# Gate 7 finished before group 5 is turned, and SSM groups 6 and 7 used last in the output projection

## The chip, the core and the metric

The kernel runs on one core of one Trainium2 chip. The metric is the device time of one execution in microseconds (us). Three runs of the kernel before gave 777.24, 779.81 and 781.50 us, median 779.81 us. TensorE (PE) does the matrix products and transposes, ScalarE (ACT) and VectorE (DVE) do elementwise work from SBUF and PSUM, GpSimd (POOL) does elementwise work on SBUF alone, and SyncE (SP) issues the weight transfers.

## The reference, cut to what matters

The whole kernel is a two-layer decoder trunk over 256 tokens of width 1024: a Mamba-2 SSD mixer with a gated feed-forward block, then dilated attention with another one. The change touches the end of the mixer only:

```
z, xbc, dt  = split(h @ w_in)
xs, B, C    = silu(conv(xbc) + conv_b)            # 8 groups: xs 256 wide, B and C 128 wide
y           = ssd(xs, dt, a, B, C) + xs * d_skip  # per chunk of 128 tokens:
              #   cb = C B^T;  y_diag = (cb * decay) (xs*dt);  y_off = C * state of the chunk before
y           = y * silu(z)                         # the gate
y           = y * rsqrt(mean(y*y over its group)) * norm_w
x           = x + y @ w_out                       # 2048 -> 1024
```

Each group has 256 of the 2048 channels of y, which are two of the 16 blocks of 128 over which `y @ w_out` sums. Blocks 12 and 13 are group 6, blocks 14 and 15 are group 7.

## The kernel before

All products are taken in three terms of split fp32 operands: high times high, high times low, low times high. Weights come as 1 MB blocks into a ring of three raw buffers; ACT casts each half to its high part (`split`, line 96, tile wh) and DVE subtracts to get the low part (line 98, tile wl), both in rings of six. PE's instructions run in the order in which the code is written; on ACT, DVE, POOL and SP a scheduler sets one order at build time, and each of these engines then works through its own list in that order.

The SSM loop runs over groups g = 0 to 7. In each turn PE makes xs (`conv_mm(g, "xs")`), B and C (`conv_mm(g, "bc")`), and in the odd turns 1, 3, 5 and 7 also one gate tile of 256 channels (`ZAT`), in two halves of 24 products (`z_mm(g, 0)` and `z_mm(g, 1)`, lines 290 to 292) that `z_post` sends through a Silu. The other steps of a group are spread over later turns:

- `ssd_b(g)`: PE transposes xs (tile px, line 542), DVE makes xdt and xd from it, POOL the third part of xdt (line 551).
- `ssd_a(g)`: PE makes C B^T (tile pg, lines 519 and 520) from B and C after their Silu (line 416), ACT copies it to gs (lines 524, 525).
- `ssd_m(g)`: POOL multiplies the decay tile dec by gs in two halves (line 531).
- `ssd_c(g)`: PE makes yo and py (lines 560 and 565, py from dec), then DVE line 567, POOL line 570, DVE line 571, POOL line 572 (times the gate), ACT line 575 (squares), DVE 576, POOL 578 (the power -0.5) and ACT line 580 (times the result) give the normed tile y2.
- `ssd_d(g)`: PE turns y2 (tile pt, line 588), ACT and DVE make the high and low part yy from it (lines 186 and 187), the operand of the output projection.

In turn 7 PE does xs, half of bc, `ssd_d(4)`, `ssd_c(5)`, the other half of bc, `ssd_b(6)`, `ssd_a(6)`, then `z_mm(7, 0)`, `ssd_d(5)`, `ssd_c(6)`, `z_mm(7, 1)`, and after the loop `ssd_b(7)` and `ssd_a(7)`. `ssd_d(6)`, `ssd_c(7)` and `ssd_d(7)` are hung into the output projection as hooks.

`res_proj` does the output projection. Its first four output tiles run together: for each half of the 16 blocks it goes tile by tile and does one step for each block that isn't in the list `late`; a step is three products (lines 666 to 668). The blocks in `late` come last, block by block over the four tiles. Hooks are called after so many steps, or ahead of a late block (`"k12"`). So before, with blocks 14 and 15 late, there are 56 steps and then 8 late ones; `ssd_d(6)` comes after step 20, `ssd_c(7)` after 24, `ssd_d(7)` after 52.

Of the kernel before, what the change touches and what calls it, by code (L numbers as in the profile page):

```python
# [16 lines left out]
NG = 8  # L17
# [10 lines left out]
ZAT = {1: 4, 3: 5, 5: 6, 7: 7}  # L28
# [25 lines left out]
def trunk(ctx, tc, a, out):  # L54
# [428 lines left out]
    yy = []  # L483
# [28 lines left out]
    def z_post(g):  # L512
        seq(out=gate(g), in_=sts[g]["poz"], func=AF.Silu)
# [23 lines left out]
    def ssd_b(g):  # L537
        st = sts[g]
        px = ps.tile([128, 2, T], F32, tag="t1", name="px")
        for c in range(2):  # L540
            for i in range(2):
                PE.transpose(px[:, c, i * 128:i * 128 + 128], st["xs"][:, i, c * 128:c * 128 + 128], ident)
        h4 = slice(4 * g, 4 * g + 4)
        xdt = wk.tile([128, 3, T], F32, tag="B", bufs=3, name="xdt")
        DVE.tensor_tensor(out=hd(xdt[:, 0:2, :]), in0=hd(px),
                          in1=dts[:, :, h4].unsqueeze(3).to_broadcast([128, 2, 4, 64]), op=ALU.mult)
        xd = wk.tile([128, 2, T], F32, tag="B", bufs=3, name="xd")
        DVE.tensor_tensor(out=hd(xd), in0=hd(px),
                          in1=P("dskip")[:, h4].unsqueeze(1).unsqueeze(3).to_broadcast([128, 2, 4, 64]),
                          op=ALU.mult)  # L550
        POOL.tensor_tensor(out=hd(xdt[:, 2:3, :]), in0=hd(xdt[:, 0:1, :]),
                           in1=ea[:, 32 + 4 * g:36 + 4 * g].unsqueeze(1).unsqueeze(3)
                           .to_broadcast([128, 1, 4, 64]), op=ALU.mult)
        st["xdt"], st["xd"] = xdt, xd

    def ssd_c(g):
        st = sts[g]
        d, xdt, xd, gs = dec[g], st["xdt"], st["xd"], st["gs"]
        po = ps.tile([128, 512], F32, tag="t4", name="yo")[:, :T]
        PE.matmul(po, lhsT=gs[:, 2, :], rhs=xdt[:, 2, :], start=True, stop=True)  # L560
        py = ps.tile([128, 2, T], F32, tag="t2", name="py")
        for c in range(2):
            for j in range(4):
                f = slice(64 * j, 64 * j + 64)
                PE.matmul(py[:, c, f], lhsT=d[:, j, c, :], rhs=xdt[:, c, f], start=True, stop=True)  # L565
        y2 = act.tile([128, 2, T], F32, tag=f"dec{g}", name="y2")
        DVE.tensor_tensor(out=hd(y2[:, 1:2, :]), in0=hd(po.unsqueeze(1)),
                          in1=ea[:, 4 * g:4 * g + 4].unsqueeze(1).unsqueeze(3).to_broadcast([128, 1, 4, 64]),
                          op=ALU.mult)
        POOL.tensor_tensor(out=xd[:, 1, :], in0=xd[:, 1, :], in1=y2[:, 1, :], op=ALU.add)  # L570
        DVE.tensor_tensor(out=xd, in0=py, in1=xd, op=ALU.add)
        POOL.tensor_tensor(out=y2, in0=xd, in1=gate(g), op=ALU.mult)
        sm = wk.tile([128, 2], F32, tag="sm", name="sm")
        for c in range(2):
            ACT.activation(out=xd[:, c, :], in_=y2[:, c, :], func=AF.Square, accum_out=sm[:, c:c + 1])
        DVE.tensor_scalar(out=sm, in0=sm, scalar1=1.0 / 256, scalar2=GEPS, op0=ALU.mult, op1=ALU.add)
        rs = wk.tile([128, 2], F32, tag="rs", name="rs")
        POOL.tensor_tensor(out=rs, in0=sm, in1=nhalf, op=ALU.pow)
        for c in range(2):
            ACT.activation(out=y2[:, c, :], in_=y2[:, c, :], func=AF.Copy, scale=rs[:, c:c + 1])  # L580
        st["y2"] = y2

    def ssd_d(g):
        st = sts[g]
        y2, pt = st["y2"], ps.tile([128, 2, T], F32, tag="t5", name="pt")
        for i in range(2):
            for c in range(2):
                PE.transpose(pt[:, i, c * 128:c * 128 + 128], y2[:, c, i * 128:i * 128 + 128], ident)
        y = act.tile([128, 4, T], F32R, tag=f"dec{g}", name="yy")
        for i in range(2):  # L590
            hi_lo(y[:, 2 * i, :], y[:, 2 * i + 1, :], pt[:, i, :], P("ssm_norm")[:, 2 * g + i:2 * g + i + 1])
        yy.append(y)
# [5 lines left out]
    for g in range(NG):  # L598
        for i in range(2):
            conv_mm(g, "xs", i)  # L600
        conv_post(g, "xs")
        conv_silu(g, "xs")
        conv_mm(g, "bc", 0)
        if g == 0:
            chunk_sums()
            decay_load(0)
            decay_load(1)
        if g > 2:
            ssd_d(g - 3)
        if g > 1:  # L610
            ssd_c(g - 2)
        conv_mm(g, "bc", 1)
        conv_post(g, "bc")
        if g and g % 2 == 0:
            decay_load(g)
            decay_load(g + 1)
        if g % 2 == 0:
            decay(g, sts[g]["end"])
            decay(g + 1, sts[g]["end"])
        if g:  # L620
            ssd_b(g - 1)
            ssd_a(g - 1)
            ssd_m(g - 1)
        conv_silu(g, "bc")
        if g == 0:
            seq(out=ea, in_=acs[:, 32:96], func=AF.Exp)
        if g % 2 == 0:
            decay_exp(g)
            decay_exp(g + 1)
        if g in ZAT:  # L630
            z_mm(ZAT[g], 0)
            if g == NG - 1:
                ssd_d(g - 2)
                ssd_c(g - 1)
            z_mm(ZAT[g], 1)
            z_post(ZAT[g])
    ssd_b(NG - 1)
    ssd_a(NG - 1)
    ssd_m(NG - 1)

    def res_proj(w, nk, operand, late, S, first=2, hooks={}):

        done = [0] * KT
        po, units = {}, {}

        def step(n, k):  # L650
            wh, wl = units[n, k // 8]
            c = slice((k % 8) * 128, (k % 8) * 128 + 128)
            shared, wide = n < first > 2, n >= (first if first > 2 else 0) and nk > AH
            if n not in po:
                po[n] = po[n - 1] if shared and n % 2 else acc_bank()
            y, p = operand(k), po[n]
            st, sp = done[n] == 0, done[n] == nk - 1
            done[n] += 1
            if wide:
                PE.matmul(p.rearrange("p c t -> p (c t)"), lhsT=wh[:, c], rhs=y.rearrange("p c t -> p (c t)"),  # L660
                          start=st, stop=False, skip_group_check=True)
                PE.matmul(p[:, 1, :], lhsT=wl[:, c], rhs=y[:, 0, :], start=False, stop=sp,  # L662
                          skip_group_check=True)
            else:

                o = n % 2 if shared else 0
                for q, (l, x) in enumerate(((wh, 0), (wh, 1), (wl, 0))):
                    PE.matmul(p[:, o, :], lhsT=l[:, c], rhs=y[:, x, :], start=st and q == 0 and not o,  # L668
                              stop=sp and q == 2, skip_group_check=True)
            if sp and shared:  # L670
                if n % 2:
                    for q in range(2):
                        finish(n - 1 + q, [p[:, q, :]])
            elif sp:
                finish(n, [p[:, q, :] for q in range(1 + wide)])

        def finish(n, ys):
            x = X[:, n, :]
            for y in ys:
                DVE.tensor_tensor(out=x, in0=y, in1=x, op=ALU.add)  # L680
            S.add(n)

        n0, steps = 0, 0
        while n0 < KT:
            m = first if n0 == 0 else 2
            tiles = range(n0, n0 + m)
            last = late if n0 == 0 else []
            for b in range(0, nk, 8):
                for p in range(n0 // 2, (n0 + m) // 2):
                    units[2 * p, b // 8], units[2 * p + 1, b // 8] = W.get(w, p, b)  # L690
                for n in tiles:
                    for k in range(b, min(b + 8, nk)):
                        if k not in last:
                            step(n, k)
                            steps += 1
                            hooks.get(steps, int)()
            for k in last:
                hooks.get(f"k{k}", int)()
                for n in tiles:
                    step(n, k)  # L700
            n0 += m

    S = Stream(["ffn_norm0"])
    res_proj("w_out", 16, lambda k: yy[k // 2][:, k % 2 * 2:k % 2 * 2 + 2, :], [14, 15], S,
             first=4, hooks={20: lambda: ssd_d(NG - 2), 24: lambda: ssd_c(NG - 1), 52: lambda: ssd_d(NG - 1)})


    def ffn(L, S, nxt):
# [251 lines left out]
    S = Stream(["ffn_norm1"])  # L960
# [209 lines left out]
```

## Time and profile before

| | |
|---|---|
| three runs, median (range) | 779.81 us (777.24 to 781.50) |
| the profiled execution's own time | 777.25 us |
| its span, first to last instruction | 775.5 us |
| PE busy (share of the span) | 761.5 us (98%) |
| DVE, ACT, POOL busy | 604.4, 470.1, 146.2 us |
| granted TensorE clock, mean | 0.997 of full speed (2.4 GHz) |

The span lies 1.75 us below the time of its own execution. Matmuls are pipelined: one of 256 columns is shown with 0.28 us though the next one starts 0.12 us later, so what a stretch costs is read from starts, not from the sum of durations. "Idle before" in a row counts from the shown end of the instruction ahead.

### The profile page before, as it was taken

Reading aid. Unit: us, or ns where it says so; the run is one execution under the profiler, and the core shown is the slowest. Engines: PE = TensorE matmul, PEld = TensorE weight load, DVE = VectorE, ACT = ScalarE, POOL = GpSimd, SP = SyncE. Lnnn points to the kernel's source line nnn. Section 1 sums busy time; section 2 is a strip of 40 time slices with the busy share of each in tenths; the row PEclk is TensorE's granted clock in tenths of the full one; section 3 lists DMA queues with packets and bytes.
Section 4 is the critical chain, followed back from the end, with each engine's and each line's share of the span. In section 5 each row is a group of like instructions: output and inputs, shape, how many; then the busy total and the mean of one; then the engine's idle time right before and its main releaser. Section 6 shows DMA issues by size and latency. Waiting matters only on the chain.

```text
span 775.5 us, 14630 instructions
## 1 busy us (share of the span) xinstructions
PE 761.5 (98%) x5832; PEld 721.9 (93%) x5832; DVE 604.4 (78%) x1008; ACT 470.1 (61%) x793; POOL 146.2 (19%) x142
## 2 busy tenths in 40 slices
PE   8999999989999999999999999999999999999996
PEld 7899999989989999999888998989999999999885
DVE  5989988887496999887677598777587999888452
ACT  6757777775566676565556446556376767655331
POOL 0003626354216100000111132111125200000000
PEclk9999999999999999999999999999999999999998
DMA  8584753434173565545556554253234565554621
GB/s 308 212 300 170 283 174 110 164 109 158 61 272 110 173 233 202 207 151 173 184 200 236 194 189 147 101 187 118 105 115 158 191 224 212 184 197 141 220 75 54
DMA packets 22772, 135.72 MB, mean 175 GB/s; under 512 B 2544, under 2 KB 3600, under 8 KB 8624
## 3 DMA queue, kind: packets, MB, share of 16 engines
q1 hardware_dynamic: 21216, 130.03, 48.2%
q10 hardware_dynamic: 1488, 4.75, 1.8%
q8 instruction: 46, 0.75, 0.4%
q14 instruction: 22, 0.18, 0.1%
HBM read 133.17 MB, written 1.61 MB: 174 GB/s over the span
## 4 chain that ended last, share of the span: by engine, by line
PE 89%; DVE 4%; issue 2%; ACT 2%; DMA 1%; POOL 1%; SPq 0%; POOLq 0%; DVEq 0%
PE po L270 18%; PE po L271 17%; PE po L272 17%; PE po L660 7%; PE po L668 4%; PE po L662 4%; PE fo L1030 2%; PE fo L1028 2%; PE fo L1029 2%; PE py L565 2%; DVE wl L98 2%; PE po L290 1%; PE po L291 1%; PE po L292 1%; DMA raw<-w_z 1%
## 5 line engine op out<-in xcount | busy, mean ns | idle before, releaser
L98 DVE TENSOR_TENSOR wl<-raw,wh 128x1024 fp32r<-128x1024 f32 (+1 forms) x238 | 296.2, 1250 | 77.9 <-ACT wh L96 73.8
L96 ACT CAST wh<-raw 128x1024 fp32r<-128x1024 f32 (+1 forms) x238 | 245.0, 1040 | 184.3 <-PE po L271 99.1
L270 PE MATMUL po<-xnh,wh 128*128 128x256 f32 x800 | 226.6, 283 | 0.0
L272 PE MATMUL po<-xnh,wl 128*128 128x256 f32 x800 | 226.1, 283 | 0.0
L271 PE MATMUL po<-xnl,wh 128*128 128x256 f32 x800 | 225.3, 282 | 0.0
L270 PEld LDWEIGHTS po<-xnh,wh 128*128 128x128 f32 x800 | 150.9, 189 | 0.4 <-issue 0.2
L271 PEld LDWEIGHTS po<-xnl,wh 128*128 128x128 f32 x800 | 151.0, 189 | 0.0
L272 PEld LDWEIGHTS po<-xnh,wl 128*128 128x128 f32 x800 | 150.1, 188 | 0.1
L270 PE MATMUL po<-xh,wh 128*128 128x256 f32 x400 | 114.7, 287 | 0.0
L271 PE MATMUL po<-xl,wh 128*128 128x256 f32 x400 | 113.0, 282 | 0.5 <-DVE xl L187 0.5
L272 PE MATMUL po<-xh,wl 128*128 128x256 f32 x400 | 113.1, 283 | 0.0
L314 DVE SCALAR_TENSOR_TENSOR cv<-po,prm,cv 128x255 f32<-128x255 f32 (+2 forms) x232 | 106.2, 477 | 5.4 <-ACT cv L310 2.8
L270 PEld LDWEIGHTS po<-xh,wh 128*128 128x128 f32 x400 | 76.1, 190 | 1.6 <-issue 1.5
L271 PEld LDWEIGHTS po<-xl,wh 128*128 128x128 f32 x400 | 76.1, 190 | 0.7 <-DVE xl L187 0.7
L272 PEld LDWEIGHTS po<-xh,wl 128*128 128x128 f32 x400 | 75.8, 190 | 0.0
L660 PE MATMUL po<-gp,wh 128*128 128x512 f32 x176 | 61.4, 392 | 0.0
L230 POOL TENSOR_TENSOR sqacc<-sqacc,sq 128x256 f32<-128x256 f32 x21 | 21.4, 1019 | 211.5 <-ACT sq L229 211.2
L662 PE MATMUL po<-gp,wl 128*128 128x256 f32 x176 | 49.3, 280 | 0.0
L660 PEld LDWEIGHTS po<-gp,wh 128*128 128x128 f32 x176 | 33.0, 187 | 7.5
L1028 PE MATMUL fo<-wh,gp 128*128 128x512 f32 x88 | 34.5, 392 | 0.0
L1030 PE MATMUL fo<-wl,gp 128*128 128x512 f32 x88 | 34.5, 392 | 0.0
L1029 PE MATMUL fo<-wh,gp 128*128 128x512 f32 x88 | 34.5, 392 | 0.0
(226 smaller groups left out, 1283.0 us busy)
## 6 DMA issues: line engine op xcount, KB each, us to landing
raw<-w_up SPq DMA_DIRECT2D x44, 1024.0 KB, 4.8
raw<-w_down SPq DMA_DIRECT2D x18, 1024.0 KB, 4.8
raw<-w_xs SPq DMA_DIRECT2D x8, 1024.0 KB, 6.2
raw<-w_bc SPq DMA_DIRECT2D x8, 1024.0 KB, 5.5
raw<-w_out SPq DMA_DIRECT2D x8, 1024.0 KB, 4.9
raw<-w_q SPq DMA_DIRECT2D x8, 1024.0 KB, 5.1
raw<-w_z SPq DMA_DIRECT2D x6, 1024.0 KB, 6.0
dec<-rows ACTq DMA_DIRECT2D x8, 512.0 KB, 5.3
```

The lines of the kernel that those rows point to most:

```text
L96: ACT.copy(out=wh[:, :n], in_=raw)
L98: DVE.tensor_tensor(out=wl[:, :n], in0=raw, in1=wh[:, :n].bitcast(F32), op=ALU.subtract)
L270: PE.matmul(po, lhsT=wh, rhs=xh, start=start, stop=False, **kw)
L271: PE.matmul(po, lhsT=wh, rhs=xl, start=False, stop=False, **kw)
L272: PE.matmul(po, lhsT=wl, rhs=xh, start=False, stop=stop, **kw)
L314: r = DVE.scalar_tensor_tensor(out=dst[:, i, s:], in0=u[:, i, :T - s], scalar=w[i][:, taps - 1 - s:taps - s], in1=dst[:, i, s:], op0=ALU.m ...
L660: PE.matmul(p.rearrange("p c t -> p (c t)"), lhsT=wh[:, c], rhs=y.rearrange("p c t -> p (c t)"), start=st, stop=False, skip_group_check=True)
L662: PE.matmul(p[:, 1, :], lhsT=wl[:, c], rhs=y[:, 0, :], start=False, stop=sp, skip_group_check=True)
L668: PE.matmul(p[:, o, :], lhsT=l[:, c], rhs=y[:, x, :], start=st and q == 0 and not o, stop=sp and q == 2, skip_group_check=True)
L1028: PE.matmul(po[c], lhsT=x[:, 0, t], rhs=wh[:, o], start=k == 0, stop=False)
L1029: PE.matmul(po[c], lhsT=x[:, 1, t], rhs=wh[:, o], start=False, stop=False)
L1030: PE.matmul(po[c], lhsT=x[:, 0, t], rhs=wl[:, o], start=False, stop=k == FT - 1)
```

## The change

Two edits, with every instruction of the computation kept. In turn 7 both halves of gate 7 are made together, and `ssd_d(5)` and `ssd_c(6)` come behind them, ahead of `ssd_b(7)`. In the output projection blocks 12 and 13 join the late ones, and the three hooks move: `ssd_c(7)` still after step 24 and now first, `ssd_d(6)` after step 30, `ssd_d(7)` ahead of late block 12. There are now 48 steps and then 16 late ones.

```diff
-        if g in ZAT:
+        if g in ZAT and g < NG - 1:
             z_mm(ZAT[g], 0)
-            if g == NG - 1:
-                ssd_d(g - 2)
-                ssd_c(g - 1)
             z_mm(ZAT[g], 1)
             z_post(ZAT[g])
+    z_mm(7, 0)
+    z_mm(7, 1)
+    z_post(7)
+    ssd_d(NG - 3)
+    ssd_c(NG - 2)
     ssd_b(NG - 1)
     ssd_a(NG - 1)
     ssd_m(NG - 1)
...
-    res_proj("w_out", 16, lambda k: yy[k // 2][:, k % 2 * 2:k % 2 * 2 + 2, :], [14, 15], S,
-             first=4, hooks={20: lambda: ssd_d(NG - 2), 24: lambda: ssd_c(NG - 1), 52: lambda: ssd_d(NG - 1)})
+    res_proj("w_out", 16, lambda k: yy[k // 2][:, k % 2 * 2:k % 2 * 2 + 2, :], [12, 13, 14, 15], S,
+             first=4, hooks={24: lambda: (ssd_c(NG - 1),), 30: lambda: (ssd_d(NG - 2),), "k12": lambda: (ssd_d(NG - 1),)})
```

PE between the two halves of gate 7, before (y2_1996 is the normed tile of group 5, po_2061 the gate's bank):

```order
L291 MATMUL po_2061<-wh_1947,xnl_335 128x256
L292 MATMUL po_2061<-wl_1949,xnh_334 128x256
L588 MATMUL pt_2096<-cst_76,y2_1996 128x128 x4
L560 MATMUL yo_2106<-xdt_2047,gs_2055 128x256
L565 MATMUL py_2108<-xdt_2047,dec_1838 128x64 x8
L290 MATMUL po_2061<-wh_1943,xnh_334 128x256
L291 MATMUL po_2061<-wh_1943,xnl_335 128x256
```

The same place of PE in the changed kernel, behind the last product of the gate's second half:

```order
L291 MATMUL po_2061<-wh_1947,xnl_335 128x256
L292 MATMUL po_2061<-wl_1949,xnh_334 128x256
L588 MATMUL pt_2121<-cst_76,y2_1996 128x128 x4
L560 MATMUL yo_2131<-xdt_2047,gs_2055 128x256
L565 MATMUL py_2133<-xdt_2047,dec_1838 128x64 x8
L542 MATMUL px_2155<-cst_76,cv_1930 128x128 x4
L519 MATMUL pg_2165<-cv_2033 128x256
L520 MATMUL pg_2165<-cv_2033 128x128
L670 MATMUL po_2193<-yy_1070,wh_2064 128x256 x2
```

The turning of group 5 and yo and py of group 6 stand 24 products later, and px and pg of group 7 follow them directly.

ACT from the norm of group 5 on, before (cv is B and C of group 7, y_2117 group 6, zp gate 7):

```order
L580 ACTIVATE y_1996<-y_1996,rs 128x256 x2
L525 COPY gs<-pg 128x128
L96 CAST wh<-raw 128x1024
L186 ACTIVATE yy<-pt,prm 128x256 x2
L416 ACTIVATE cv<-cv 128x512
L96 CAST wh<-raw 128x1024
L575 ACTIVATE xd,sm<-y_2117 128x256 x2
L416 ACTIVATE zp<-po 128x2x256
```

ACT from the same place in the changed kernel (y_2142 is group 6):

```order
L580 ACTIVATE y_1996<-y_1996,rs 128x256 x2
L525 COPY gs<-pg 128x128
L96 CAST wh<-raw 128x1024 x3
L186 ACTIVATE yy<-pt,prm 128x256
L416 ACTIVATE cv<-cv 128x512
L416 ACTIVATE zp<-po 128x2x256
L186 ACTIVATE yy<-pt,prm 128x256
L524 COPY gs<-pg 128x256
L525 COPY gs<-pg 128x128
L575 ACTIVATE xd,sm<-y_2142 128x256 x2
```

Two more casts of weights stand ahead of the Silu of B and C of group 7.

POOL at groups 6 and 7, as a difference (y_2117 and y_2142 are group 6 before and now, y_2288 and y_2278 group 7; the dec rows and xdt are group 7):

```order
-L570 TENSOR_TENSOR xd<-xd,y_2117 128x256
-L572 TENSOR_TENSOR y_2117<-xd,zp 128x512
+L570 TENSOR_TENSOR xd<-xd,y_2142 128x256
+L531 TENSOR_TENSOR dec<-dec,gs 128x512
+L551 TENSOR_TENSOR xdt<-xdt,ea 128x256
+L531 TENSOR_TENSOR dec<-dec,gs 128x512
+L572 TENSOR_TENSOR y_2142<-xd,zp 128x512
 L578 TENSOR_TENSOR rs<-sm,nhalf 128x2
-L551 TENSOR_TENSOR xdt<-xdt,ea 128x256
-L531 TENSOR_TENSOR dec<-dec,gs 128x512 x2
```

The three POOL instructions of group 7 now stand inside group 6's chain, between lines 570 and 572.

## Rows read from the trace of the kernel before

**Rows 1.** Waits of PE over the span, longest group: total us, times, longest

```profile
PE pt L588 <- ACT y L580: 2.1, 1, 2.1
```

**Rows 2.** Timeline of PE, turn 7: start us, duration us, line, tiles, count [idle before]

```profile
168.92 0.36 PE L290 MATMUL po<-wh,xnh 128*128 128x256 f32 x1
...
174.07 0.95 PE L588 MATMUL pt<-cst,y 128*128 128x128 f32 x4 [2.09 <-ACT y L580]
...
177.36 0.36 PE L290 MATMUL po<-wh,xnh 128*128 128x256 f32 x1
...
180.29 0.60 PE L542 MATMUL px<-cst,cv 128*128 128x128 f32 x4
180.73 0.60 PE L519 MATMUL pg<-cv 128*128 128x256 f32 x2
...
181.30 0.49 PE L668 MATMUL po<-yy,wh 128*128 128x256 f32 x2
```

**Rows 3.** Timeline of PE: group 4 turned, group 5's yo and py, no wait

```profile
162.38 0.60 PE L588 MATMUL pt<-cst,y 128*128 128x128 f32 x4
...
164.95 0.36 PE L270 MATMUL po<-xnh,wh 128*128 128x256 f32 x1
```

**Rows 4.** Timeline of ACT, turn 7 and output projection

```profile
173.51 0.91 ACT L580 ACTIVATE y<-y,rs 128x256 f32<-128x256 f32 x2 [0.26 <-POOL rs L578]
...
174.47 1.05 ACT L96 CAST wh<-raw 128x1024 fp32r<-128x1024 f32 x1
175.42 0.47 ACT L186 ACTIVATE yy<-pt,prm 128x256 fp32r<-128x256 f32 x1
176.51 0.47 ACT L186 ACTIVATE yy<-pt,prm 128x256 fp32r<-128x256 f32 x1 [0.62 <-DVE yy L187]
176.89 0.63 ACT L416 ACTIVATE cv<-cv 128x512 f32<-128x512 f32 x1
...
184.16 0.90 ACT L580 ACTIVATE y<-y,rs 128x256 f32<-128x256 f32 x2
...
198.83 0.91 ACT L580 ACTIVATE y<-y,rs 128x256 f32<-128x256 f32 x2 [1.34 <-POOL rs L578]
```

**Rows 5.** Timeline of DVE, turn 7 and output projection

```profile
176.39 0.47 DVE L314 SCALAR_TENSOR_TENSOR cv<-po,prm,cv 128x253 f32<-128x253 f32 x1
...
177.66 0.42 DVE L567 TENSOR_TENSOR y<-yo,ea 128x256 f32<-128x256 f32 x1 [0.80 <-PE py L565]
...
179.55 3.43 DVE L98 TENSOR_TENSOR wl<-raw,wh 128x1024 fp32r<-128x1024 f32 x2
...
184.29 1.23 DVE L98 TENSOR_TENSOR wl<-raw,wh 128x1024 fp32r<-128x1024 f32 x1
...
193.03 0.42 DVE L567 TENSOR_TENSOR y<-yo,ea 128x256 f32<-128x256 f32 x1
```

**Rows 6.** Timeline of POOL, groups 6 and 7

```profile
173.44 2.51 POOL L531 TENSOR_TENSOR dec<-dec,gs 128x512 f32<-128x512 f32 x2
...
179.78 2.12 POOL L572 TENSOR_TENSOR y<-xd,zp 128x512 f32<-128x512 f32 x1 [0.87 <-DVE xd L571]
...
183.80 0.62 POOL L551 TENSOR_TENSOR xdt<-xdt,ea 128x256 f32<-128x256 f32 x1
...
185.40 3.53 POOL L531 TENSOR_TENSOR dec<-dec,gs 128x512 f32<-128x512 f32 x2 [0.98 <-ACT gs L524]
```

**Rows 7.** Timeline of PE in the output projection, at the hooks

```profile
188.59 0.60 PE L588 MATMUL pt<-cst,y 128*128 128x128 f32 x4
188.94 0.48 PE L668 MATMUL po<-yy,wh 128*128 128x256 f32 x2
...
190.46 0.60 PE L560 MATMUL yo<-xdt,gs 128*128 128x256 f32 x2
...
192.59 0.48 PE L668 MATMUL po<-yy,wh 128*128 128x256 f32 x2
...
202.74 0.60 PE L588 MATMUL pt<-cst,y 128*128 128x128 f32 x4
```

## The prediction, made before the changed kernel ran

> **What bounds the kernel now.** I read the busy times and the list of what PE waited for first, then the timelines of PE, ACT, DVE and POOL over turn 7 and the output projection. PE is busy nearly all the time (98% in the table above), so a change is worth what it adds to or takes from PE's starts. PE's longest wait of the whole execution is the one of the turning of group 5 (pt) for ACT's last step of the norm, line 580 [rows 1]. It lies between the two halves of gate 7, which is where the first edit works.
>
> The row says 2.09 us; the starts say more. From the first product of the gate's first half to the first of its second half pass 177.36 - 168.92 = 8.44 us [rows 2]. The 24 products of a half take 180.29 - 177.36 = 2.93 us [rows 2], and pt, yo and py take 164.95 - 162.38 = 2.57 us where PE doesn't wait [rows 3]. So 8.44 - 2.93 - 2.57 = 2.94 us are lost there. The shown wait is shorter because it leaves out the turning's own slow start (its second half needs the second scaled half of y2) and a short wait of py for dec. The rest of the projection has no wait of PE, so 2.94 us is all there is to win.
>
> **First edit, at the gate.** Nothing is added or removed, and up to 168.92 both kernels are alike on each engine. Now both halves run first: 168.92 + 2 x 2.93 = 174.78. Then comes pt; its y2 is ready at 173.51 + 0.91 = 174.42 [rows 4], 0.36 us ahead, so this wait goes. pt, yo and py end at 174.78 + 2.57 = 177.35. The last half of dec, which py needs, is done at 173.44 + 2.51 = 175.95 [rows 6], and py is the last part of that stretch, so I charge nothing. px takes 180.73 - 180.29 = 0.44 us, to 177.79.
>
> What is late next is pg. It needs B and C of group 7 after their Silu, and ACT now has three casts in a row ahead of the Silu instead of one. The first starts at 174.47, and the step from it to the next ACT instruction was 0.95 us [rows 4]: casts at 174.47, 175.42 and 176.37 (the gate weights they replace are free by 174.78), yy at 177.32, the Silu 0.38 us behind (176.89 - 176.51) at 177.70, done 0.63 us later at 178.33 [rows 4]. Its other input is the last tap of the convolution on DVE, which now stands behind one low part of weights: from the end of the first cast, 175.52, plus 1.23 us [rows 5], plus up to 0.43 us if it has to wait until dec is done at 175.95, plus 0.47 us for the tap [rows 5]: 177.65 at the latest, so ACT's queue decides. pg waits from 177.79 to 178.33, a new wait of 0.54 us. pg takes 181.30 - 180.73 = 0.57 us [rows 2], and the output projection starts at 178.90 in place of 181.30: **2.40 us earlier**. From below this term is 2.94 us (no wait of pg); from above 1.9 us, if the Silu comes half a cast later still. Behind the Silu stand Silu of gate 7, half of yy, and gs; none of these is wanted by PE before the hooks.
>
> **Second edit, in the projection.** The steps are the same number; only the order changes. One step takes (202.74 - 192.59) / 28 = 0.3625 us, `ssd_c` 2.13 us and `ssd_d` 0.35 us [rows 7]. New times on PE: `ssd_c(7)` at 178.90 + 24 x 0.3625 = 187.60, `ssd_d(6)` at 187.60 + 2.13 + 6 x 0.3625 = 191.91, `ssd_d(7)` at 178.90 + 48 x 0.3625 + 2.13 + 0.35 = 198.78. Do their inputs come in time?
>
> Group 6's y2: DVE's line 567 comes at about 179.3 (tap done 177.65, one low part of 1.23 us, one yy of about 0.4). Before, line 580 ended 184.16 + 0.90 - 177.66 = 7.40 us after it [rows 4, 5]; that gives 186.7. But POOL now does group 7's two halves of dec and its xdt between lines 570 and 572: 3.53 + 0.62 us, less the 0.87 us that POOL idled there anyway [rows 6], so +3.28: 190.0. These are durations beside low parts on DVE; without them the halves take 2.51 for 3.53, and line 572, of the same shape as one half, about 1.25 for 2.12 [rows 6]: 188.1. I take the middle, 189.1. PE wants it at 191.91: covered by 1.9 us at the least.
>
> Group 7's y2: DVE has three low parts ahead of line 567 of group 7, the last of them behind two casts that ACT does after line 580 of group 6: 189.1 + about 2.0 + 1.23 = 192.3 (191.3 to 193.2). At the pace of before line 567 would come 193.03 - 190.46 = 2.57 us after yo [rows 5, 7], at 190.17; so it is 2.1 us late (1.1 to 3.0). Before, y2 was ready 198.83 + 0.91 - 190.46 = 9.28 us after yo [rows 4, 7]: 196.88 + 2.1 = 199.0 (198.0 to 199.9), and PE wants it at 198.78. So a **wait of 0.2 us**, between 0 and 1.1. Behind `ssd_d(7)` stand 8 late steps, 2.9 us, before the first that needs group 7: ACT and DVE have two yy each in that time, about 2 us, so no further wait.
>
> The weights: in both kernels all first-half units of the four tiles are used up in the first 32 steps, and the second-half ones to the last late block, so what frees them and the transfers behind them moves with PE. From the first tile pair behind these four on, the two kernels are the same program 2.2 us apart, and PE has only short waits there, none for a transfer, so I let the gain stand to the end.
>
> Where DVE and POOL lie side by side the trace shows both longer: line 572 took 2.12 us while two low parts took 3.43 in place of 2 x 1.23 [rows 5, 6]. The Trainium skill ("SBUF — State Buffer", section "SBUF: two separate sides") says why: a DVE instruction with two SBUF inputs and a POOL instruction take one port pair in turn, and the later one is blocked for the whole of the earlier. The trace agrees: 2.12 + 1.2 us add up to the stretch. The rule speaks against this change, which puts three POOL instructions into the chain that DVE's low parts interrupt; by it each meeting could cost the chain up to a whole low part, 1.23 us, and the wait at `ssd_d(7)` would be 1 to 2 us in place of 0.2.
>
> **Sum.** 2.40 - 0.2 = 2.2 us, from an own time of 777.25: 775.05 us. That execution lies 2.56 us under the median of the runs shown, so on their scale 779.81 - 2.2 = **777.6 us**. The case's own range is a gain of 0.8 to 2.94 us: 776.9 to 779.0.
>
> **Rivals.**
> 1. *All comes back.* pg finds its Silu ready and y2 of group 7 is in time: 2.94 us, 776.9 us. For it: the inputs miss by only 0.54 and 0.2 us. Against it: three casts in order on ACT can't be shorter than their rows.
> 2. *The wait only moves.* The Silu is held until PE stands at pg as long as it stood at pt, some 2 us more than forecast, or `ssd_d(7)` takes the rest: 0 to 0.8 us gained, 779.4 us. For it: pg already waits, and ACT and DVE each work through one list. Against it: all inputs of the Silu are dated by rows to within 0.5 us.
> 3. *Slower: the norm of group 7 is late.* POOL and DVE collide along the chain from line 567 of group 6 to line 580 of group 7. It decides once y2 of group 7 comes after 198.78 + 2.40 = 201.2, which is 2.2 us beyond the forecast and 1.3 us beyond its late end. Each collision costs 0.5 to 0.9 us (half of 3.53 - 2.51; 2.12 - 1.25) [rows 6]; four more than the late end has, on lines 570 and 572 of group 7 and the low parts around them, give 199.9 + 3.4 = 203.3, a wait of 4.5 us and 2.1 us lost: 781.9 us. For it: ACT, DVE and POOL all wait for one another in this chain. Against it: before, the same chain ran beside low parts and had its collisions already in the 9.28 us.
>
> **Chances.** Forecast 0.70, all back 0.12, wait moved 0.12, slower 0.06. The three runs of before lie 4.3 us apart, 0.55%, so 0.5% (3.9 us) is about what can be told from no change. No case reaches 3.9 us by its own working; only scatter added to a gain of 2 to 3 us does (0.09), or a chain later than rival 3's (0.05); within 0.5%: 0.86. The range takes the cases from 776.9 to 779.4 and the scatter of a median, about 2 us below and 1 us above them: 774.8 to 780.4.
>
> **What would show it.** Right: PE's wait at pt of group 5 is gone, a wait of about half a us stands at pg for the Silu, the projection starts near 178.9, and any wait at pt of group 7 is under a us. Wrong: a wait of over 1 us at pg, at pt of group 6 or at pt of group 7; a start of the projection later than 180; or a difference that arises behind the projection, where I expect none.

## The result and the profile after

The changed kernel takes 774.96 us (median of 7 runs, 774.56 to 776.20) against 780.16 us of the kernel before (7 runs, 777.24 to 781.50): ratio 0.9934, 95% interval 0.9916 to 0.9951. In a second comparison (`after_again` below) it is 0.9936 (0.9924 to 0.9948). So it is faster by about 5 us, and the time lies inside the predicted range (774.8 to 780.4), 0.16 us above its low end. But the two profiles differ by only 2 us: own time 777.25 to 775.28 us, span 775.5 to 773.5 us. Where the other 3 us come from is the main question of the experiments.

The profile first. Waits of PE over the span of the changed kernel (total us, times, longest), which answer to [rows 1]:

```profile
PE poz L290 <- ACT wh L167: 1.8, 2, 1.2
...
PE pg L519 <- ACT cv L416: 0.3, 1, 0.3
```

The wait of pt for line 580 is gone from the list. A wait of pg for the Silu is new. All the others of the list stand in that of the kernel before too; those for the first weights (tile poz, in the first 20 us) differ in length from one profiled execution to the next: 0.8 us for wh there, 1.8 us here.

Timeline of PE of the changed kernel over turn 7 and the projection (start us, duration us, line, tiles, count, idle before), answering to [rows 2, 7]:

```profile
169.26 0.36 PE L290 MATMUL po<-wh,xnh 128*128 128x256 f32 x1
...
174.97 0.60 PE L588 MATMUL pt<-cst,y 128*128 128x128 f32 x4
175.41 0.60 PE L560 MATMUL yo<-xdt,gs 128*128 128x256 f32 x2
175.84 2.09 PE L565 MATMUL py<-xdt,dec 128*128 128x64 f32 x16
177.77 0.61 PE L542 MATMUL px<-cst,cv 128*128 128x128 f32 x4
178.69 0.70 PE L519 MATMUL pg<-cv 128*128 128x256 f32 x2 [0.32 <-ACT cv L416]
179.23 0.38 PE L520 MATMUL pg<-cv 128*128 128x128 f32 x2
179.37 0.48 PE L670 MATMUL po<-yy,wh 128*128 128x256 f32 x2
...
199.36 0.60 PE L588 MATMUL pt<-cst,y 128*128 128x128 f32 x4
...
205.55 0.39 PE L662 MATMUL po<-yy,wh 128*128 128x512 f32 x1
```

The first row is the first product of the gate; it starts at 169.26, since this execution was 0.34 us behind the one profiled before when it came there. The next rows give the whole of turn 7's tail and of the first four tiles: the busy time of each engine in the stretches from there to the projection and from there to the first step of the next tile pair (us, then PE, PEld, DVE, ACT, POOL busy with their counts, granted clock, DMA share, GB/s; PEld is PE's loading of weights):

```profile
169.26:179.37 10.11, 9.79 (x81) 9.33 (x80) 9.58 (x17) 9.57 (x21) 5.08 (x5) 1.00 0.20 56
179.37:205.55 26.18, 26.18 (x221) 26.13 (x220) 12.54 (x20) 10.98 (x25) 9.62 (x10) 1.00 0.46 156
```

The same for the kernel before: from the end of its wait at pt to px, and over the first four tiles.

```profile
174.07:180.29 6.22, 5.99 (x46) 5.61 (x47) 4.38 (x9) 3.88 (x7) 3.13 (x4) 1.00 0.00 0
181.30:207.48 26.18, 26.18 (x221) 26.13 (x220) 13.10 (x18) 12.16 (x26) 8.29 (x9) 1.00 0.47 162
```

From the gate to the projection it took 181.30 - 168.92 = 12.38 us before [rows 2] and takes 10.11 now: 2.27 us gained. The first four tiles take 26.18 us in both, with PE busy from end to end, so nothing was gained or lost in the projection. In both profiled executions the granted clock is 1.00 in all these stretches.

Timeline of ACT of the changed kernel, answering to [rows 4]: the casts ahead of the Silu, and the end of group 7's norm.

```profile
174.81 2.94 ACT L96 CAST wh<-raw 128x1024 fp32r<-128x1024 f32 x3
177.65 0.47 ACT L186 ACTIVATE yy<-pt,prm 128x256 fp32r<-128x256 f32 x1
178.02 0.62 ACT L416 ACTIVATE cv<-cv 128x512 f32<-128x512 f32 x1
...
187.74 0.91 ACT L580 ACTIVATE y<-y,rs 128x256 f32<-128x256 f32 x2
...
197.42 0.91 ACT L580 ACTIVATE y<-y,rs 128x256 f32<-128x256 f32 x2
```

Timeline of POOL of the changed kernel, answering to [rows 6], and the low part of weights that DVE makes beside it: group 7's dec inside group 6's chain.

```profile
180.44 1.29 POOL L531 TENSOR_TENSOR dec<-dec,gs 128x512 f32<-128x512 f32 x1
181.69 0.61 POOL L551 TENSOR_TENSOR xdt<-xdt,ea 128x256 f32<-128x256 f32 x1
182.26 2.27 POOL L531 TENSOR_TENSOR dec<-dec,gs 128x512 f32<-128x512 f32 x1
184.49 1.29 POOL L572 TENSOR_TENSOR y<-xd,zp 128x512 f32<-128x512 f32 x1
```

```profile
181.77 1.61 DVE L98 TENSOR_TENSOR wl<-raw,wh 128x1024 fp32r<-128x1024 f32 x1
```

Of the four POOL rows only one half of dec was lengthened by the low part (2.27 us for 1.29). Group 6's norm ends at 188.65, group 7's at 198.33, and PE turns group 7 at 199.36, 1.03 us after that.

### The profile page after: what moved, and what is told of

Its sections match the earlier page's. It is cut to its first block, busy times and chain, and to the rows that moved or that the text cites. A ratio compares the mean times of both kernels' runs of the same rounds, so it can differ in the third digit from the quotient of the medians.

```text
span 773.5 us, 14630 instructions
## 1 busy us (share of the span) xinstructions
PE 759.7 (98%) x5832; PEld 720.0 (93%) x5832; DVE 603.3 (78%) x1008; ACT 469.9 (61%) x793; POOL 146.7 (19%) x142
## 4 chain that ended last, share of the span: by engine, by line
PE 89%; DVE 4%; issue 2%; ACT 2%; DMA 1%; POOL 1%; SPq 0%; POOLq 0%; DVEq 0%
PE po L270 18%; PE po L271 17%; PE po L272 17%; PE po L662 7%; PE po L670 4%; PE po L664 4%; PE fo L1030 2%; PE fo L1032 2%; PE fo L1031 2%; DVE wl L98 2%; PE py L565 1%; DMA raw<-w_z 1%; PE po L290 1%; PE po L291 1%; PE po L292 1%
```

## The experiments

Two theories stood against each other. **A**: the change is worth the wait that the profiles show, some 2.3 us, and the other 3 us are scatter of the kernel before. **B**: in most executions of the kernel before TensorE's clock falls after the wait in turn 7, and the one profiled execution was one of the others.

**b_again: the kernel before, run again.** No edit.

> The kernel before, unchanged, run again, because its seven times spread over 4.3 us while the changed kernel's spread over 1.6 us, and the one profiled execution was among its shortest. Theory A (only the wait): the change is worth the 1.9 to 2.4 us that the two profiles show, and the rest of the measured difference of 5.2 us is scatter of the kernel before that has nothing to do with the wait; then its times lie again between 777 and 782 us, and its granted clock is near 0.997 in long and short executions alike. Theory B (the clock): in most executions of the kernel before the wait of PE in turn 7 is followed by a stretch at the lower of the two clock levels, which the profiled execution did not have; then executions of 780 us and more show a lower mean granted clock than those of 777 us, by 0.003 to 0.005.

Measured: 779.81 us (12 runs), ratio 0.9997 (0.9979 to 1.0015) to the 34 runs of the kernel before beside it. The list of executions gives the mean granted clock of each. Taking the 46 of this comparison and 14 of the second one, there are two groups and nothing between: 11 executions from 776.83 to 777.68 us with a clock of 0.997 or 0.999, and 49 from 779.47 to 783.39 us with 0.988 to 0.995. Their medians are 777.11 and 780.17 us, 3.06 us apart. The execution profiled before (777.25 us, 0.997) is of the short kind. (The seven of the result have no clock on record; one of them, 778.08 us, lies between the groups.) This fits B and not A; it doesn't yet show where the clock falls, and both profiled executions of the kernel before are of the short group.

**proj_only: the second edit alone.**

```diff
-             ..., [14, 15], S,
-             first=4, hooks={20: lambda: ssd_d(NG - 2), 24: lambda: ssd_c(NG - 1), 52: lambda: ssd_d(NG - 1)})
+             ..., [12, 13, 14, 15], S,
+             first=4, hooks={24: lambda: (ssd_c(NG - 1),), 30: lambda: (ssd_d(NG - 2),), "k12": lambda: (ssd_d(NG - 1),)})
```

> Only the second edit: four late blocks and the moved hooks, with gate 7 split as before. PE's wait in turn 7 stays (2.1 us shown), and no wait of PE in the projection goes, since there was none. Theories A and B alike: 1.000 of the kernel before within 0.15%, with the same scatter. If it is faster by 2 us or more, the order inside the projection has a worth of its own.

Measured: 780.16 us, ratio 1.0009 (0.9994 to 1.0023). Alone the second edit is worth nothing, as expected. Its 12 executions fall into the same two groups: one of 777.01 us with 0.997, eleven from 779.67 to 783.14 us with 0.988 to 0.994. The profiled one (780.12 us, clock 0.994) was one of the long ones, and as its turn 7 is that of the kernel before, it shows the place. Busy times of the engines by stretch, of this kernel (columns as above; the granted clock stands third from the end):

```profile
168.96:174.10 5.14, 3.05 (x27) 2.85 (x25) 4.75 (x10) 4.85 (x13) 3.16 (x4) 1.00 0.18 77
174.10:177.00 2.90, 2.83 (x15) 2.48 (x15) 2.21 (x5) 2.28 (x6) 1.87 (x2) 0.74 0.00 0
177.00:180.00 3.00, 3.00 (x15) 3.00 (x15) 0.82 (x2) 0.56 (x2) 0.54 (x1) 0.50 0.00 0
180.00:183.19 3.19, 3.19 (x21) 3.19 (x19) 2.60 (x3) 1.04 (x1) 2.32 (x2) 0.64 0.16 21
183.19:186.00 2.81, 2.81 (x25) 2.76 (x24) 2.76 (x5) 2.75 (x8) 1.31 (x3) 1.00 0.84 312
```

The clock is at its upper level, 2.4 GHz, through the wait, falls to 1.2 GHz after it (0.50 of full speed) and is back at the upper level by 183.19. The timeline of PE of the same execution shows what that costs:

```profile
174.10 0.94 PE L588 MATMUL pt<-cst,y 128*128 128x128 f32 x4 [2.09 <-ACT y L580]
174.88 0.60 PE L560 MATMUL yo<-xdt,gs 128*128 128x256 f32 x2
175.32 3.54 PE L565 MATMUL py<-xdt,dec 128*128 128x64 f32 x16
178.61 0.56 PE L290 MATMUL po<-wh,xnh 128*128 128x256 f32 x1
...
180.89 0.41 PE L291 MATMUL po<-wh,xnl 128*128 128x256 f32 x1
181.10 0.41 PE L292 MATMUL po<-wl,xnh 128*128 128x256 f32 x1
...
183.19 0.38 PE L542 MATMUL px<-cst,cv 128*128 128x128 f32 x2
```

The same wait of 2.09 us stands ahead of pt as in [rows 2]; then the products come 0.21 us apart instead of 0.12. From pt to px pass 9.09 us, where it was 180.29 - 174.07 = 6.22 us [rows 2]: 2.87 us more in the same stretch, which is nearly the whole gap of 3.06 us between the two groups.

**filler: PE kept busy in the wait, nothing taken off the path.**

```diff
             if g == NG - 1:
+                fill = ps.tile([128, 512], F32, tag="t1", name="fill")
+                for _ in range(9):
+                    PE.matmul(fill[:, :128], lhsT=ones, rhs=ones, start=True, stop=True)
                 ssd_d(g - 2)
```

> The kernel before with nine products of ones by ones (128 columns each, about 1.95 us of PE) put where PE waits for group 5's norm, into a bank that nobody reads. It takes no wait away from the path: the turning starts at about 174.1 either way. Theory A: same as the kernel before, within 0.1%, with the same scatter of some 4 us. Theory B: PE isn't idle there, the clock stays at its upper level in all executions, and the kernel is about 3 us faster than the kernel before, near 777.3 us, with a spread of under 2 us.

Measured: 777.06 us (12 runs, 776.68 to 779.30), ratio 0.9964 (0.9949 to 0.9980), clock 0.995 to 0.999. Adding work to the kernel before makes it 3 us faster. Its profile shows the products in the place of the wait:

```profile
173.92 2.17 PE L635 MATMUL fill<-ones 128*128 128x128 f32 x18
176.17 0.95 PE L588 MATMUL pt<-cst,y 128*128 128x128 f32 x4
```

The turning still starts slowly (0.95 us) and py still waits for dec, so the path through the norm is the old one; in the stretch behind, the granted clock is 1.00. Theory A would have had no gain here. That the loss of 3 us goes with PE's idleness in this wait is shown, since filling it takes the loss away and leaves the path.

Two parts of theory B's expectation missed: the spread is 2.6 us and not under 2, and the clock did not stay up everywhere. The profiled execution is the longest of the twelve (779.30 us), and its clock fell at another place, among PE's waits for the first weights:

```profile
10.00:15.00 5.00, 3.14 (x8) 2.22 (x9) 3.58 (x5) 4.87 (x10) 1.27 (x1) 0.78 1.01 372
15.00:20.00 5.00, 5.00 (x21) 4.03 (x21) 4.96 (x9) 3.22 (x4) 0.00 (x0) 0.88 1.02 402
```

It begins the gate at 171.03, 2.1 us later than the kernel before, after longer waits there and the fall; that is about what it lies above the median. So a low mean clock alone doesn't say that the fall stands in turn 7.

**gate_only: the first edit alone.**

```diff
-             ..., [12, 13, 14, 15], S,
-             first=4, hooks={24: ..., 30: ..., "k12": ...})
+             ..., [14, 15], S,
+             first=4, hooks={20: lambda: ssd_d(NG - 2), 24: lambda: ssd_c(NG - 1), 52: lambda: ssd_d(NG - 1)})
```

(the changed kernel with the old list and hooks)

> Only the first edit: gate 7 whole ahead of the turning of group 5; the output projection as before, with groups 6's turning after step 20, group 7's yo and py after 24, group 7's turning after 52, blocks 14 and 15 late. The projection starts at about 179, as in the changed kernel, so group 6's turning would come at 179.3 + 7.3 = 186.6, while its y2 is ready at about 188.6: a new wait of PE of about 2 us, which gives back most of the 2.3. Theory A: same as before within 0.15%, some 779.5 us. Theory B: the new wait is as long as the old one, so the clock's loss stays as well: about 780 us. If it is instead as fast as the changed kernel, the second edit does nothing.

Measured: 776.98 us (11 runs, 776.53 to 778.16), ratio 0.9962 (0.9951 to 0.9974). The new wait is there, in the profile's row of PE at the turning of group 6:

```profile
187.59 0.95 PE L588 MATMUL pt<-cst,y 128*128 128x128 f32 x4 [1.50 <-ACT y L580]
```

but I expected the clock to fall after it, and in the profile it did not (its mean is 0.999); all 11 executions have a mean clock of 0.996 to 0.999. The longest, 778.16 us with 0.996, lies 1.2 us above the median, and no trace shows why. So the first edit alone removes the clock's loss and moves the rest of the wait; the second edit then takes away that rest, 776.98 to 774.96 us. My expectation for theory B was wrong in this: the new wait, 1.5 us and at another place, did not bring the clock down.

**after_again and two_late: does the list of late blocks matter?** `after_again` is the changed kernel with no edit. `two_late` keeps its gate and its hooks, and puts blocks 12 and 13 back among the steps:

```diff
-             ..., [12, 13, 14, 15], S,
-             first=4, hooks={24: ..., 30: ..., "k12": lambda: (ssd_d(NG - 1),)})
+             ..., [14, 15], S,
+             first=4, hooks={24: ..., 30: ..., 52: lambda: (ssd_d(NG - 1),)})
```

> The changed kernel once more, beside the variants below. Theory B (the wait, and the clock that falls after it): about 775.0 us, spread under 2 us, mean granted clock 0.997 or 0.998, because no wait of PE in the middle of the kernel is left that is over a us. Theory A (scatter that has nothing to do with the wait): a spread of some 4 us like that of the kernel before.

> The changed kernel, its gate and its hooks kept (group 7's turning after step 52), but only blocks 14 and 15 late, so that block 12 of the first tile comes 4 steps into the second half of the blocks. Group 6's yy would be wanted at about 194.6 and 195 in the changed kernel's times, and is ready at 194.2 and 197.1: a new wait of PE of about 2 us at block 13. Theory B: 777 us if the clock stays up, up to 780 where it falls after the new wait. If it is as fast as the changed kernel, making blocks 12 and 13 late is worth nothing and the moved hooks do it alone.

Measured: `after_again` 774.81 us (6 runs, 774.66 to 775.24), clock 0.997 to 0.999 in all. `two_late` 776.46 us (776.29 to 776.69), ratio to the kernel before 0.9956 (0.9944 to 0.9968). Its profile has the wait where it was expected, at the first product that needs the second half of group 6's yy:

```profile
195.96 0.90 PE L670 MATMUL po<-yy,wh 128*128 128x256 f32 x2 [1.05 <-ACT yy L186]
```

The row before it starts at 194.63, so about 1.2 us pass unused and the first products come slowly; the medians of `two_late` and `after_again` lie 1.65 us apart. The moved hooks alone would not do: group 6 has to be used late.

**long_wait: the wait made longer.** The turning of group 5 ahead of gate 7's first half in the kernel before:

```diff
         if g in ZAT:
+            if g == NG - 1:
+                ssd_d(g - 2)
             z_mm(ZAT[g], 0)
             if g == NG - 1:
-                ssd_d(g - 2)
                 ssd_c(g - 1)
```

> The kernel before with the turning of group 5 put ahead of gate 7's first half: the same work, and PE waits there about 5 us in place of 2.1, since group 5's norm isn't ready earlier; yo and py of group 6 keep their place between the halves. Theory A: the wait alone grows by 2.9 us less what py's wait gives back, some 782.5 us, scatter as before. Theory B: the same, and the clock falls after the wait in every execution and not in most: no execution in a fast group near 780, and a mean granted clock of 0.995 or lower in all.

Measured: 781.87 us (9 runs, 781.35 to 782.54), ratio 1.0031 (1.0017 to 1.0044), clock 0.991 to 0.994 in every one. PE's row at the turning, and busy times by stretch of its profile:

```profile
173.96 1.30 PE L588 MATMUL pt<-cst,y 128*128 128x128 f32 x4 [4.87 <-DVE cv L314]
```

```profile
169.00:174.00 5.00, 0.13 (x2) 0.04 (x1) 4.58 (x9) 4.73 (x12) 3.17 (x4) 0.94 0.14 61
174.00:177.00 3.00, 3.00 (x14) 2.78 (x15) 2.38 (x6) 2.38 (x6) 1.84 (x2) 0.50 0.00 0
177.00:180.00 3.00, 3.00 (x16) 3.00 (x16) 1.34 (x2) 0.47 (x1) 0.00 (x0) 0.50 0.36 63
```

The row names a step of DVE that ended at about the same moment; what pt reads is y2, whose first half ACT was scaling from 173.40. With a wait of 4.9 us the group without a fall is gone, as B said. The time grew by 1.7 us over the long group's 780.17 and not by the 2.4 that I had put on it. That py no longer waits was already in the 2.4; what gave back the rest was not looked into (the profiled executions of `long_wait` and `proj_only` lie 2.04 us apart).

**pg_later: the new wait taken away.** Group 7's pg behind step 2 of the projection, in the changed kernel:

```diff
     ssd_b(NG - 1)
-    ssd_a(NG - 1)
-    ssd_m(NG - 1)
...
-             first=4, hooks={24: lambda: (ssd_c(NG - 1),), ...
+             first=4, hooks={2: lambda: (ssd_a(NG - 1), ssd_m(NG - 1)), 24: lambda: (ssd_c(NG - 1),), ...
```

> The changed kernel with group 7's product of B and C (pg), and POOL's product behind it, hung behind step 2 of the output projection, so that PE does 0.7 us of steps where it waits now (0.6 us at pg for ACT's Silu). Both theories: 0.3 to 0.6 us faster than the changed kernel, 774.4 to 774.7 us, if group 7's norm is still in time: it now stands ready at 198.3 and PE comes at 199.4. If POOL's order makes the norm later by over 1 us, no gain.

Measured: 774.20 us (6 runs, 773.93 to 774.34), ratio to the kernel before 0.9926 (0.9913 to 0.9939). It lies 0.6 us under `after_again` on the same chip, and the two sets of times don't overlap. PE's rows there:

```profile
177.28 0.61 PE L542 MATMUL px<-cst,cv 128*128 128x128 f32 x4
177.65 0.48 PE L668 MATMUL po<-yy,wh 128*128 128x256 f32 x2
...
178.44 0.59 PE L519 MATMUL pg<-cv 128*128 128x256 f32 x2
```

Steps fill the half us that pg waited, pg has no wait in its row, and group 7's norm is still in time. This is the fastest version that was run.

## Why the prediction was right, and what it missed

The time lies in the range, but by luck. Each case of the forecast ends at 776.9 us or later; 774.96 us is reached only through the 2 us that the range allows below them for the scatter of a median. What filled this allowance is not scatter but a loss of clock that the forecast had put at nothing.

- **The lost time at pt.** 2.94 us were read from starts as the most that could come back. The stretch from the gate to the projection fell by 2.27 us where 2.40 were forecast. "2.94 us is all there is to win" held for the profiled execution alone.
- **The new wait at pg.** Forecast 0.54 us, from three casts in a row on ACT. Counted by starts it is 178.69 - 177.77 - 0.44 = 0.48 us beyond px, and ACT's rows run as laid out, the Silu behind three casts and one half of yy. `pg_later` gave 0.6 us back when it was filled. The 0.13 us between 2.40 and 2.27 are the sum of four small terms: the gate's two halves take 174.97 - 169.26 = 5.71 us and not 5.86, from pt to px pass 177.77 - 174.97 = 2.80 us and not 2.57, the wait is 0.48 us and not 0.54, and pg takes 179.37 - 178.69 = 0.68 us and not 0.57. Of the 0.23 us between pt and px a part is a term that the forecast put at nothing: py had begun at 175.84, the last half of dec was done at 176.32 (POOL's dec rows start at 173.78 and take 2.54 us), and PE's weight loads for py pause there for about 0.1 us.
- **The norm of group 6.** Forecast ready between 188.1 and 190.0, measured 188.65; on the forecast's clock, 0.34 us less, near the early end.
- **The norm of group 7.** Forecast 0.2 us too late (between 0 and 1.1); it was 1.03 us early, so the term is nothing and not 0.2. The middle between the collisions of before and none was too dark: one of the four POOL rows was lengthened, by 0.98 us. Rival 3 asked for several such collisions. By the Trainium skill's rule of the shared port pair ("SBUF — State Buffer", section "SBUF: two separate sides") the later of the two instructions is blocked for the whole of the earlier. The one collision that there was agrees: the low part of 181.77 ends at 183.38, and the half of dec ends 184.53 - 183.38 = 1.15 us after that, close to the 1.29 us that it takes alone.
- **Sum within the profile.** Forecast 2.2 us; measured 2.27 us between the gate and the next tile pair, 2.0 us of span because this execution came 0.34 us later to the gate. Within the profile the mechanism and its size are those of the forecast.
- **The step that failed.** "That execution lies 2.56 us under the median of the runs shown, so on their scale 779.81 - 2.2", and "No case reaches 3.9 us by its own working". The first took the distance from the median for scatter, and the second followed from it. `b_again`, `proj_only` and `filler` show that it was no scatter: in 49 of 60 executions the wait that the change removes costs about 3.06 us more than its own length, in clock, and the profiled execution was of the kind of the other 11, where it doesn't. The true sum on the scale of the median is 2.3 + 3.0 = 5.3 us, against 5.2 measured. With it the forecast would have been 774.5 us, and the chance of more than 0.5% far above 0.09.
- **What could have told.** The profile of before had the wait and, in the runs shown, 777.24 us beside 779.81 and 781.50, with nothing in the trace to explain 2.5 us. The Trainium skill ("TensorE: Matmul & The Clock Gate", section "HAM oscillation — how this bites in real kernels") says of a kernel whose PE waits 3 to 5 us for transfers between bursts that it is throttled again in each wait and starts the next burst at the low level. This case agrees that the clock falls about a wait, here one of 2.09 us, but in `proj_only` the burst began at the upper level and the fall came inside it. The profiled execution of before shows no fall behind its wait (1.00 in its rows above), and the forecast left it out. As a rival a fall would have been worth 2.9 us here: `proj_only` shows it with 0.50 in the row, and in `long_wait` the mean clock was 0.991 to 0.994 in every execution.

The decomposition, from medians: kernel before 780.1, without the clock's fall 777.1 (`filler`), without the fall and with a shorter wait at another place 777.0 (`gate_only`), without the wait 774.9, and without the wait at pg 774.2.

## What to carry to other kernels

A wait of TensorE like this one, 2 us in the middle of dense work, is to be priced with its own length and, as a rival, with the products behind it at half clock; the profile of one execution may show either case, so compare the mean granted clock over all executions before its distance from the median is called scatter. Work that can be put into the wait is then worth more than the wait; here even work that does nothing gave back 3 us. When a step moves behind a block of products, look for the engine whose list it shares with weight casts: here the next wait stood there, and a few products of what follows filled it.

## What the runs showed of the hardware

The fall did not come at a fixed point of the wait. In the long execution of `proj_only` the clock was 1.00 up to 174.10, where PE's wait of 2.09 us had already ended; 0.74 over the next 2.90 us and 0.50 behind them put the fall at about 175.5 (an estimate from these two rows), while PE was busy again. In `long_wait` it fell before the wait ended at 173.96: 0.94 over the 5 us up to 174.00 are some 0.6 us at the low level (an estimate from that row).

How often it falls differs between the waits, counted by time and mean clock: 9 of 9 executions with the wait of 4.9 us, 49 of 60 with that of 2.1 us, none of 11 with that of 1.5 us in `gate_only`, where two executions have 0.996 and no trace. The waits differ in place as well as in length, and `filler` had a fall between 10 and 20 us, where PE's longest wait was 1.4 us, so these counts are no rule by length. What decides between the 49 and the 11 was not tried.
